# Splitting two weight halves with one instruction in the expert stage of a three-layer kernel

## The chip, the cores and the metric

The kernel runs on one core of a Trainium2 chip. The metric is the device time of one execution in microseconds. The kernel before was timed three times, and the median counts. A separate execution was taken with the hardware profiler; all durations below come from that one.

## The reference

One sequence of 256 tokens with 1024 features passes through three layers: a hybrid layer with four token mixers and a dense feed-forward block, a retention layer with a dense feed-forward block, and a Fourier layer with a mixture of eight experts. The last block is the one that matters here:

```python
logits = t @ w_router                          # 256 x 8
top_val, top_idx = lax.top_k(logits, 2)        # two experts for each token
top_w = softmax(top_val)
for e in range(8):
    out = out + gates[:, e:e + 1] * ((silu(t @ w_gate[e]) * (t @ w_up[e])) @ w_down[e])
```

Each expert has a gate and an up matrix of 1024 x 3584 and a down matrix of 3584 x 1024, all in float32. Its weights are 44 MB, and those of all eight, 352 MB, are most of what the kernel reads.

## The kernel before, in words

All weights lie in memory as units of 128 x 2048 float32 numbers, 1 MiB each, in the order of their use. There are `NU` units; the last 8 x 42 belong to the experts. SyncE's queue (SP) loads unit after unit into raw places, tiles named `raw`: six from the start, four more before the second dense block (`raw2p`), two more before the Fourier mixer (`raw3p`) and two more before the experts (`raw4p`). In the expert stage the tile `xT` serves as one more. So 15 units can be loaded ahead there. A raw place is given back, and its next load issued, when VectorE (DVE) has finished the second half of the unit.

TensorE multiplies in a rounded float32 format, so each weight is split into a rounded part and a remainder. `split()` does that for half a unit, 128 x 1024: ScalarE (ACT) copies `raw` to `wh` with rounding (L128), then DVE writes `wl = raw - wh` (L129). `wh` and `wl` come from the pool `wp` with four buffers each, so four halves at most are split and not yet used up. The list `wq` holds halves that wait for use. `half()` first splits one more half (unless told `ahead=False`), then takes the oldest from `wq`.

The orders of TensorE (PE) and SP are as the code writes them. Those of ACT and DVE are made by a scheduler from priorities, and each engine then runs its list in order.

The experts: `experts()` (from L1115) walks seven strips of 512 hidden columns. A strip takes 12 halves: four for the gate projection (`gate_strip`, L1142 to L1144), four for the up projection (`up_strip`), four for the down projection of the strip before (`down`). In `gate_strip` every half is fetched by a `nexth()` of its own; in `up_strip` and `down` two are fetched by `pair()`, which splits one half before the matmuls and one after. ScalarE takes the silu of the gate strip (`sg`, L1177), DVE multiplies it by the up strip (`h`, L1184), `turn()` transposes that on PE (`sd`, L1194 or L1196), and ACT and DVE split the result into `hx` (L1200, L1201). An expert with at most 64 tokens takes the packed form for up, down and the transposes: both parts of the tokens' numbers lie side by side in one stationary operand (L1139 and L1144), 4 matmuls for a half and not 6. The gate strips always take 6.

Around the experts, `gather()` builds the tokens of the next expert: selection matrices `so` on DVE (L1082), `rows` on PE (L1093), `xs` on ACT (L1095), `tokens_of` on PE (L1100), `ex` on ACT and DVE (L1102, L1103), and `rest` on PE (L1108, L1110), which reads the row scale `rcol` and feeds `rsl` and `sot` (L1111, L1112). These steps are hooked into the last seven halves of the expert before. `result()` splits an expert's output into `y`, and `combine()` adds it to `acc` during the next expert.

Of the kernel before, what the change touches and what calls it, by code (L numbers as in the profile page):

```python
# [9 lines left out]
F32 = mybir.dt.float32  # L10
F32R = mybir.dt.float32r
I32 = mybir.dt.int32
AF = mybir.ActivationFunctionType
ALU = mybir.AluOpType
AX = mybir.AxisListType

P = 128
# [5 lines left out]
E = 8  # L23
FE = 3584
NFE = FE // P
UN = 2048
UE = 42
# [36 lines left out]
def kernel(  # L64
# [10 lines left out]
    nc = tc.nc  # L75
    NU = ws_d.shape[0]
    WB = 4
    HP = 300
    HQ = 512
    HU = UN // 2  # L80

    NRAW, R2N, R3N, R4N = 6, 4, 2, 2
    const = ctx.enter_context(tc.tile_pool(name="const", bufs=1))
    rawp = ctx.enter_context(tc.tile_pool(name="rawp", bufs=NRAW))
    wp = ctx.enter_context(tc.tile_pool(name="wp", bufs=WB))
    psp = ctx.enter_context(tc.tile_pool(name="psp", bufs=2, space=bass.MemoryType.PSUM))
    ctx.enter_context(tc.manual_schedule(engines={mybir.EngineType.PE, mybir.EngineType.SP}))

# [1 line left out]
    raw = []  # L90
    wq = []
# [18 lines left out]
    def more_room(name, n):  # L110
        pool = ctx.enter_context(tc.tile_pool(name=name, bufs=n))
        for _ in range(n):
            fetch(pool)

    half_ = [0, 0]

    def split(scales=None, between=None):


        if not raw or (half_[1] == H_F2 and scales is None):  # L120
            return
        half_[1] += 1
        r = raw[0][0][:, half_[0] * HU:(half_[0] + 1) * HU]
        wh = wp.tile([P, HU], F32R, tag="wh", name="wh")
        wl = wp.tile([P, HU], F32R, tag="wl", name="wl")
        if scales is None:
            for o in (slice(0, HQ), slice(HQ, HU)) if half_[1] == 1 else (slice(0, HU),):
                nc.scalar.activation(out=wh[:, o], in_=r[:, o], func=AF.Copy)  # L128
                nc.vector.tensor_tensor(out=wl[:, o], in0=r[:, o], in1=wh[:, o].bitcast(F32), op=ALU.subtract)  # L129
                if between is not None and o.start == 0:  # L130
                    between()
        else:
            for t in range(2):
                o = slice(t * 512, t * 512 + 512)
                nc.scalar.activation(out=wh[:, o], in_=r[:, o], func=AF.Copy, scale=scales[:, t:t + 1])
                nc.vector.scalar_tensor_tensor(out=wl[:, o], in0=r[:, o], scalar=scales[:, t:t + 1],
                                               in1=wh[:, o].bitcast(F32), op0=ALU.mult, op1=ALU.subtract)
        wq.append((wh, wl))
        if half_[0]:
            fetch(raw.pop(0)[1])  # L140
        half_[0] ^= 1
# [29 lines left out]
    def half(ahead=True):  # L171

        for item in list(side):
            item[0] -= 1
            if item[0] <= 0:
                advance(item)
        if ahead:
            split()
        return wq.pop(0)
# [6 lines left out]
    def mm3T(ps, u, b, xh, xl, start, stop):  # L186
        wh, wl = u
        c = slice(b * P, (b + 1) * P)
        mm(ps, wh[:, c], xh, start=start, stop=False)  # L189
        mm(ps, wh[:, c], xl, start=False, stop=False)  # L190
        mm(ps, wl[:, c], xh, start=False, stop=stop)  # L191
# [10 lines left out]
    def unit_late(xh, xl, late=2):  # L202

        ps = [bank("mm", (P, S)) for _ in range(2)]
        us = []
        for cb in range(2):
            us.append(half())
            for k in range(KD - late):
                mm3T(ps[cb], us[cb], k, xh[:, k], xl[:, k], k == 0, False)
        for cb in range(2):  # L210
            for k in range(KD - late, KD):
                mm3T(ps[cb], us[cb], k, xh[:, k], xl[:, k], False, k == KD - 1)
        return ps

    def stripX(xh, xl, mid=None):
# [157 lines left out]
    with pa:  # L373
# [9 lines left out]
        def hilo(dst, j, src):  # L383
# [11 lines left out]
                                in1=col(C_N1, 8).unsqueeze(2).to_broadcast([P, KD, 4]), op=ALU.mult)  # L395
# [342 lines left out]
    with ExitStack() as pr:  # L738
# [120 lines left out]
        for c in range(KD):  # L859
            ps = bank("mm", (P, S))  # L860
            for j in range(16):
                if j % 8 == 0:
# [16 lines left out]
                            in1=col(C_FFN1, 8).unsqueeze(2).to_broadcast([P, KD, E]), op=ALU.mult)  # L879
    th = xh.rearrange("p (t a) s -> p t (a s)", t=2)  # L880
    tl = xl.rearrange("p (t a) s -> p t (a s)", t=2)
    if R3N:
        more_room("raw3p", R3N)
    with ExitStack() as pn:
        N = pn.enter_context(tc.tile_pool(name="N", bufs=1))
        zh = N.tile([P, KD, S], F32R, name="zh")
# [124 lines left out]
        for c in range(0, KD, 2):  # L1011
            ps, o = to_tok(xT_, c, "mm")
# [46 lines left out]


    pt.close()
    if R4N:
        more_room("raw4p", R4N)
    xT_flat = xT.rearrange("p a b -> p (a b)")
    fetch(xT_flat)
    fn = xT_flat[:, 0:D]
    with ExitStack() as pe:
# [48 lines left out]
        def experts(ex, rs, half_fn, hooks=None, n_of=None):  # L1116
# [10 lines left out]
            def nexth(**kw):  # L1127
                if hooks and n[0] in hooks:
                    hooks[n[0]]()
                n[0] += 1  # L1130
                return half_fn(**kw)
# [76 lines left out]
            def down(s, mid=None):  # L1208
                def blocks(b0):
                    pair(lambda w, packed: hi_lo(ht[s], [down_item(s, b0 + i, w[i], hf) for i in range(2) for hf in range(2)],  # L1210
                                                 packed))

                blocks(0)
                if mid is not None:
                    mid()
                if s < 6:
                    blocks(2)
                else:

                    w = [nexth() for _ in range(2)]  # L1220
                    for hf in range(2):
                        either(lambda packed: hi_lo(ht[s], [down_item(s, b, w[b - 2], hf) for b in (2, 3)], packed))
                        with tc.high_priority(HP):
                            result(hf)

            res = []

            def result(hf):
                y = G2.tile([P, 2, 512], F32R, tag="hx", name="y")
                yh, yl = y[:, 0], y[:, 1]  # L1230
                nc.scalar.activation(out=yh, in_=pd[hf], func=AF.Copy)
                nc.vector.tensor_tensor(out=yl, in0=pd[hf], in1=yh.bitcast(F32), op=ALU.subtract)
                res.append((yh, yl))
# [30 lines left out]
        for i in (0, 2, 1, 3):  # L1264
            nxt[3][i]()
        finish_rms()
        last = None
        for e in range(E):
            ex, sot, rs, _ = nxt
# [34 lines left out]
        with tc.tile_pool(name="O", bufs=1) as O:  # L1304
            ecur = O.tile([P, E], F32, name="ecur")
            emask = O.tile([P, E], F32, name="emask")
            epos = O.tile([P, 2], F32, name="epos")
            egts = O.tile([P, 2], F32, name="egts")
            etmp = O.tile([P, 2, E], F32, name="etmp")
            with tc.If(n_over[0] + n_over[1] > 0):  # L1310

                nc.vector.tensor_copy(out=ecur, in_=io8)
                with tc.For_i(0, E, 1) as ev:
                    nc.vector.tensor_scalar(out=emask, in0=ecur, scalar1=-8.0, scalar2=None, op0=ALU.is_equal)
                    for src, dst in ((pos, epos), (gts, egts)):
                        nc.vector.tensor_tensor(out=etmp, in0=src, in1=emask.unsqueeze(1).to_broadcast([P, 2, E]), op=ALU.mult)
                        nc.vector.tensor_reduce(out=dst, in_=etmp, axis=AX.X, op=ALU.add)
                    nc.vector.tensor_scalar(out=epos, in0=epos, scalar1=float(-P), scalar2=None, op0=ALU.add)
                    cnt_ = [0]
                    cur_ = []  # L1320

                    def ohalf(ahead=True):
                        i, h = divmod(cnt_[0], 2)
                        if h == 0:
                            t = rawp.tile([P, UN], F32, tag="raw", name="oraw")
                            nc.sync.dma_start(t, ws_d[bass.ds(ev * UE + (NU - E * UE + i), 1)].rearrange("a p n -> p (a n)"))
                            cur_[:] = [t]
                        r = cur_[0][:, h * HU:(h + 1) * HU]
                        wh = wp.tile([P, HU], F32R, tag="wh", name="owh")
                        wl = wp.tile([P, HU], F32R, tag="wl", name="owl")  # L1330
                        nc.scalar.activation(out=wh, in_=r, func=AF.Copy)
                        nc.vector.tensor_tensor(out=wl, in0=r, in1=wh.bitcast(F32), op=ALU.subtract)
                        cnt_[0] += 1
                        return wh, wl

                    oex, osot, ors, steps = gather(lambda t: epos[:, t:t + 1], lambda t: epos[:, t:t + 1])
                    for f in steps:
                        f()
                    combine(experts(oex, ors, ohalf), osot, lambda t: egts[:, t:t + 1])
                    nc.vector.tensor_scalar(out=ecur, in0=ecur, scalar1=-1.0, scalar2=None, op0=ALU.add)  # L1340
                for hf in range(2):
                    out_sumsq(hf)
                out_rms()
# [172 lines left out]
```

## Time and profile before

| what | value |
|---|---|
| time, median of 3 (all: 1871.12, 1874.76, 1873.32) | 1873.32 us |
| time of the profiled execution | 1872.74 us |
| its span, first to last instruction | 1871.0 us |
| PE busy | 1817.4 us (97%) |
| DVE busy | 1482.0 us (79%) |
| ACT busy | 1210.6 us (65%) |
| mean DMA rate over the span | 270 GB/s |

The page gives each engine's busy time over the whole span. These are means over stages that differ: up to about 895 us the three layers' dense work, then the experts to about 1856 us, then the final norm. The expert stage is read from windows, one for an expert. The packed form of an expert shows in its number of matmuls. A line group of the trace gives a mean duration, which for DVE and ACT is longer than the distance of two such instructions that follow each other, since the next starts before the last has ended; that distance is read from the rows of a timeline.

### The profile page before, as it was taken

Reading aid. Unit: us, or ns where it says so; the run is one execution under the profiler, and the core shown is the slowest. Engines: PE = TensorE matmul, PEld = TensorE weight load, DVE = VectorE, ACT = ScalarE, POOL = GpSimd, SP = SyncE. Lnnn points to the kernel's source line nnn. Section 1 sums busy time; section 2 is a strip of 40 time slices with the busy share of each in tenths; the row PEclk is TensorE's granted clock in tenths of the full one; section 3 lists DMA queues with packets and bytes.
Section 4 is the critical chain, followed back from the end, with each engine's and each line's share of the span. In section 5 each row is a group of like instructions: output and inputs, shape, how many; then the busy total and the mean of one; then the engine's idle time right before and its main releaser. Section 6 shows DMA issues by size and latency. Waiting matters only on the chain. (4 is left out here: it accounts for less than half of the span.)

```text
span 1871.0 us, 28740 instructions
## 1 busy us (share of the span) xinstructions
PE 1817.4 (97%) x10890; PEld 1574.5 (84%) x10890; DVE 1482.0 (79%) x1855; ACT 1210.6 (65%) x1484; POOL 158.2 (8%) x154
## 2 busy tenths in 40 slices
PE   8999999999999999999999999999999999999997
PEld 7999999999888999998777887777777788888885
DVE  5666676657677666656899989999999998988987
ACT  5765454455344444446787777888878777777775
POOL 2302122211111122110000000000000000000000
PEclk9999999999999999999999999999999999999999
DMA  8344544555444564544799998999999999999970
GB/s 313 140 154 168 193 178 183 181 181 197 158 150 159 189 248 184 187 170 180 295 419 377 353 367 326 411 386 377 415 354 413 381 353 364 332 356 354 343 290 36
DMA packets 71156, 505.77 MB, mean 270 GB/s; under 512 B 7888, under 2 KB 8016, under 8 KB 10320
## 3 DMA queue, kind: packets, MB, share of 16 engines
q1 hardware_dynamic: 70992, 503.53, 70.7%
q8 instruction: 110, 1.80, 0.4%
q14 instruction: 54, 0.44, 0.1%
HBM read 502.45 MB, written 1.05 MB: 269 GB/s over the span
## 5 line engine op out<-in xcount | busy, mean ns | idle before, releaser
L129 DVE TENSOR_TENSOR wl<-raw,wh 128x1024 fp32r<-128x1024 f32 (+1 forms) x906 | 1078.5, 1227 | 235.3 <-ACT wh L128 226.2
L128 ACT ACTIVATE wh<-raw 128x1024 fp32r<-128x1024 f32 (+1 forms) x906 | 922.0, 1053 | 428.9 <-PE mm L190 188.7
L189 PE MATMUL mm<-xh,wh 128*128 128x256 f32 x1248 | 357.5, 286 | 6.7 <-ACT xh L342 6.7
L1144 PE MATMUL mm<-wl,ex 128*128 128x512 f32 x896 | 356.0, 397 | 3.7 <-DVE wl L129 3.7
L190 PE MATMUL mm<-xl,wh 128*128 128x256 f32 x1248 | 355.2, 285 | 1.0 <-DVE xl L343 0.7
L191 PE MATMUL mm<-xh,wl 128*128 128x256 f32 x1248 | 354.9, 284 | 0.8 <-DVE wl L129 0.8
L1142 PE MATMUL mm<-wh,ex 128*128 128x512 f32 x672 | 270.4, 402 | 0.0
L1143 PE MATMUL mm<-wh,ex 128*128 128x512 f32 x672 | 266.1, 396 | 0.2 <-DVE ex L1103 0.2
L189 PEld LDWEIGHTS mm<-xh,wh 128*128 128x128 f32 x1248 | 237.9, 191 | 8.2 <-ACT xh L342 6.7
L190 PEld LDWEIGHTS mm<-xl,wh 128*128 128x128 f32 x1248 | 237.9, 191 | 2.4 <-DVE xl L343 2.3
L191 PEld LDWEIGHTS mm<-xh,wl 128*128 128x128 f32 x1248 | 237.7, 190 | 1.1 <-DVE wl L129 1.0
L1144 PEld LDWEIGHTS mm<-wl,ex 128*128 128x128 f32 x896 | 168.6, 188 | 54.2 <-DVE wl L129 13.7
L1144 PE MATMUL dn<-wl,hx 128*128 128x512 f32 x448 | 183.6, 410 | 12.1 <-DVE wl L129 11.9
L1143 PEld LDWEIGHTS mm<-wh,ex 128*128 128x128 f32 x672 | 126.7, 189 | 28.2 <-DVE ex L1103 0.5
L1142 PEld LDWEIGHTS mm<-wh,ex 128*128 128x128 f32 x672 | 126.6, 188 | 26.0 <-ACT wh L128 0.3
L1144 PEld LDWEIGHTS dn<-wl,hx 128*128 128x128 f32 x448 | 84.2, 188 | 55.8 <-DVE wl L129 40.1
L190 PE MATMUL mm<-hl,wh 128*128 128x256 f32 x352 | 99.8, 283 | 0.0
L191 PE MATMUL mm<-hh,wl 128*128 128x256 f32 x352 | 99.8, 283 | 0.0
L189 PE MATMUL mm<-hh,wh 128*128 128x256 f32 x352 | 99.8, 283 | 0.0
L1139 PE MATMUL dn<-wh,hx 128*128 128x512 f32 x224 | 89.2, 398 | 0.0
L1142 PE MATMUL dn<-wh,hx 128*128 128x512 f32 x224 | 88.9, 397 | 0.0
L1139 PE MATMUL mm<-wh,ex 128*128 128x512 f32 x224 | 88.7, 396 | 0.0
(400 smaller groups left out, 2500.7 us busy)
## 6 DMA issues: line engine op xcount, KB each, us to landing
raw<-in_ws_dram SPq DMA_DIRECT2D x451, 1024.0 KB, 6.3
xT<-in_ws_dram SPq DMA_DIRECT2D x22, 1024.0 KB, 7.0
raw<-in_ws_dram SPq DMA_DIRECT2D x3, 512.0 KB, 6.3
xT<-in_xT_dram SPq DMA_DIRECT2D x4, 256.0 KB, 5.4
xT<-in_xT_dram SPq DMA_DIRECT2D x1, 1024.0 KB, 8.3
out_dram<-acc SPq DMA_DIRECT2D x4, 256.0 KB, 2.1
cstA<-in_cst_dram SPq DMA_DIRECT2D x1, 576.0 KB, 9.1
raw<-in_ws_dram SPq DMA_DIRECT2D x2, 256.0 KB, 4.5
```

Source lines behind the costliest of these rows:

```text
L128: nc.scalar.activation(out=wh[:, o], in_=r[:, o], func=AF.Copy)
L129: nc.vector.tensor_tensor(out=wl[:, o], in0=r[:, o], in1=wh[:, o].bitcast(F32), op=ALU.subtract)
L189: mm(ps, wh[:, c], xh, start=start, stop=False)
L190: mm(ps, wh[:, c], xl, start=False, stop=False)
L191: mm(ps, wl[:, c], xh, start=False, stop=stop)
L1139: mm(out_, e, wh, start=first, stop=False)
L1142: mm(out_, e, wh, start=first, stop=False)
L1143: mm(out_, xk[:, P:2 * P], wh, start=False, stop=False)
L1144: mm(out_, e, wl, start=False, stop=last)
```

## The change

From the fifth half of the experts on (`H_MOE + WB`), `split()` treats a whole unit: one ACT instruction and one DVE instruction of 128 x 2048, into one of four places that stay for the whole stage, each with room for a unit's `wh` and `wl`. Two of them are the old four buffers, now one tile each (`ringh`, `ringl`), two are new (`place0`, `place1`). The call of `split()` that would have split the unit's second half does nothing. Before the experts start, `wq` is filled to six halves (a unit's two halves join together), and the next unit is split when one more unit has been used up. The raw pools `raw3p` and `raw4p`, four buffers, go. In the earlier stages halves are split as before, into the four parts of the ring. Where two halves are in use at once (`unit_late`, and the end of `down`), the second `split()` is moved behind their matmuls. The final unit is split in halves, since it is loaded in halves.

```diff
-    NRAW, R2N, R3N, R4N = 6, 4, 2, 2
+    NRAW, R2N = 6, 4
-    wp = ctx.enter_context(tc.tile_pool(name="wp", bufs=WB))
+    wp = ctx.enter_context(tc.tile_pool(name="wp", bufs=1))
+
+    ring = [wp.tile([P, WB, HU], F32R, name=f"ring{n}") for n in "hl"]
+    H_MOE = 2 * (NU - E * UE)
+    places = [[r.rearrange("p a n -> p (a n)")[:, i * UN:(i + 1) * UN] for r in ring] for i in (0, 1)]
+    if H_MOE % WB:
+        places.reverse()
...
+        if half_[1] >= H_MOE + WB:
+
+            r, pool = raw[0]
+            wide = half_[1] < 2 * NU - 2
+            if not (wide and half_[0]):
+                wh, wl = places[(half_[1] - H_MOE) // 2 % 4]
+                o = slice(0, UN) if wide else slice(half_[0] * HU, (half_[0] + 1) * HU)
+                nc.scalar.activation(out=wh[:, o], in_=r[:, o], func=AF.Copy)
+                nc.vector.tensor_tensor(out=wl[:, o], in0=r[:, o], in1=wh[:, o].bitcast(F32), op=ALU.subtract)
+                for i in range(2) if wide else half_[0:1]:
+                    wq.append((wh[:, i * HU:(i + 1) * HU], wl[:, i * HU:(i + 1) * HU]))
+                if wide or half_[0]:
+                    raw.pop(0)
+                    fetch(pool)
+            half_[0] ^= 1
+            half_[1] += 1
+            return
+        wh, wl = (r[:, half_[1] % WB] for r in ring)
         half_[1] += 1
         r = raw[0][0][:, half_[0] * HU:(half_[0] + 1) * HU]
-        wh = wp.tile([P, HU], F32R, tag="wh", name="wh")
-        wl = wp.tile([P, HU], F32R, tag="wl", name="wl")
...
-            us.append(half())
+            us.append(half(ahead=not cb))
...
+        split()
         return ps
...
-    if R3N:
-        more_room("raw3p", R3N)
...
-    if R4N:
-        more_room("raw4p", R4N)
+    wp3 = ctx.enter_context(tc.tile_pool(name="wp3", bufs=1))
+    for i in range(2):
+        places.append([wp3.tile([P, UN], F32R, name=f"place{i}{n}") for n in "hl"])
...
-                    w = [nexth() for _ in range(2)]
+                    w = [nexth(), nexth(ahead=False)]
...
+                    if half_fn is half:
+                        split()
...
         finish_rms()
+        while len(wq) < 6:
+            split()
```

PE's list is the same row for row. ACT's and DVE's lists change at three places that matter below.

Place one is a strip in the middle of an expert, on ACT. `hx` is the transposed product of the strip before, `sg` the silu of this strip's gate part, and the rows L128 or L135 are splits; a branch is the end of a packed-or-not section on PE. ACT before:

```order
L1200 ACTIVATE hx_10568<-sd_10558 128x4x128
L128 ACTIVATE wh_10596<-raw_10158 128x1024
L128 ACTIVATE wh_10621<-raw_10158 128x1024
L1177 ACTIVATE sg_10593<-mm_10535,rsl_9952 128x512
L1150 UNCONDITIONAL_BRANCH
L128 ACTIVATE wh_10627<-raw_10177 128x1024
L1150 UNCONDITIONAL_BRANCH
L128 ACTIVATE wh_10652<-raw_10177 128x1024
L128 ACTIVATE wh_10660<-raw_10212 128x1024
```

And ACT now:

```order
L1222 ACTIVATE hx_9760<-sd_9750 128x4x128
L1199 ACTIVATE sg_9779<-mm_9733,rsl_9387 128x512
L135 ACTIVATE place1h_9369<-raw_9484 128x2048
L1172 UNCONDITIONAL_BRANCH
L135 ACTIVATE ringh_64<-raw_9554 128x2048
L1172 UNCONDITIONAL_BRANCH
L135 ACTIVATE ringh_64<-raw_9579 128x2048
L1172 UNCONDITIONAL_BRANCH
L135 ACTIVATE place0h_9367<-raw_9592 128x2048
L135 ACTIVATE place1h_9369<-raw_9621 128x2048
```

Between `hx` and `sg` two half splits stood, and now none does. On DVE the same strip has six halves between `hx` and `h` and six between `h` and the next `hx`, and now three units and three units.

Place two is the end of the first expert on DVE, where the next expert's tokens (`ex`, `so`, `rsl`, `sot`) are made. DVE before:

```order
L1201 TENSOR_TENSOR hx_11268<-sd_11258,hx_11268 128x4x128
L1103 TENSOR_TENSOR ex_10002<-sd_11275,ex_10002 128x4x128
L129 TENSOR_TENSOR wl_11317<-raw_10843,wh_11316 128x1024
L1150 UNCONDITIONAL_BRANCH
L129 TENSOR_TENSOR wl_11342<-raw_10843,wh_11341 128x1024
L1103 TENSOR_TENSOR ex_10002<-sd_11347,ex_10002 128x4x128
L1150 UNCONDITIONAL_BRANCH
L129 TENSOR_TENSOR wl_11355<-raw_10876,wh_11354 128x1024
L1150 UNCONDITIONAL_BRANCH
L1111 COPY rsl_10004<-sd_11358 128x1
```

And DVE now:

```order
L1223 TENSOR_TENSOR hx_10478<-sd_10468,hx_10478 128x4x128
L1125 TENSOR_TENSOR ex_9447<-sd_10481,ex_9447 128x4x128
L1172 UNCONDITIONAL_BRANCH
L1133 COPY rsl_9449<-sd_10552 128x1
L1134 CAST sot_9448<-sd_10552 128x256
L1104 TENSOR_SCALAR so_11750<-cst_73,pos_9294 128x64
L1104 TENSOR_SCALAR so_11750<-cst_73,posu_9295 128x64
L136 TENSOR_TENSOR place1l_9370<-raw_10223,place1h_9369 128x2048
L1172 UNCONDITIONAL_BRANCH x2
L1125 TENSOR_TENSOR ex_9447<-sd_10545,ex_9447 128x4x128
```

Three half splits stood between the first `ex` and `rsl`, and now none does. At the other six handovers a unit stands before and a unit behind the first `ex`, and `rsl` comes after `y`.

Place three is the start of the first expert on DVE. The rows L311 to L318 compute the row scale `rcol` step by step, `so` selects tokens. DVE now:

```order
L314 TENSOR_SCALAR rsy_9421<-rsh_9418 128x2
L136 TENSOR_TENSOR place0l_9368<-raw_8514,place0h_9367 128x2048
L316 SCALAR_TENSOR_TENSOR rs1_9417<-rsy_9421 128x2
L1104 TENSOR_SCALAR so_9442<-cst_73,pos_9294 128x64
L317 TENSOR_TENSOR rs1_9417<-rs1_9417,rs0_9416 128x2
L1104 TENSOR_SCALAR so_9442<-cst_73,posu_9295 128x64
L318 SCALAR_TENSOR_TENSOR rsy_9421<-rs1_9417,rsy_9421 128x2
L136 TENSOR_TENSOR place1l_9370<-raw_8568,place1h_9369 128x2048
L1125 TENSOR_TENSOR ex_9385<-sd_9402,ex_9385 128x4x128
```

Before, no split stood between these rows; the first four halves of the expert were split during the Fourier layer's last matmuls, as they still are, and the next came after both `ex`.

## Rows read from the trace of the kernel before

**Rows 1.** Windows, one an expert: busy us of each engine, granted clock, DMA share, GB/s.
```profile
1010.30:1136.50 126.20, 125.73 (x560) 101.05 (x559) 113.18 (x113) 95.00 (x105) 0.00 (x0) 1.00 0.95 353
1250.30:1364.00 113.70, 108.27 (x480) 81.99 (x480) 111.42 (x112) 93.16 (x105) 0.00 (x0) 1.00 0.97 388
```

**Rows 2.** Line groups, experts: busy us, mean ns; idle before, releasers.
```profile
L129 DVE TENSOR_TENSOR wl<-raw,wh 128x1024 fp32r<-128x1024 f32 x623 | 728.3, 1221 | 59.6 <-ACT wh L128 56.1 <-PE mm L1144 0.2
L128 ACT ACTIVATE wh<-raw 128x1024 fp32r<-128x1024 f32 x624 | 626.3, 1053 | 147.1 <-PE mm L1143 83.5 <-PE dn L1142 34.6 <-PE mm L1142 12.9
...
L1201 DVE TENSOR_TENSOR hx<-sd,hx 128x512 fp32r<-128x512 f32 x56 | 38.5, 688 | 0.3
...
L1194 PE MATMUL sd<-cst,h 128*128 128x128 f32 x224 | 30.1, 278 | 4.0 <-DVE h L1184 4.0
```

**Rows 3.** Timeline of DVE over one packed strip: start us, us, engine, line, xcount.
```profile
1302.46 7.12 DVE L129 TENSOR_TENSOR wl<-raw,wh 128x1024 fp32r<-128x1024 f32 x6
1309.50 0.75 DVE L1184 SCALAR_TENSOR_TENSOR h<-mm,rsl,sg 128x512 f32<-128x512 f32 x1
1310.16 5.76 DVE L129 TENSOR_TENSOR wl<-raw,wh 128x1024 fp32r<-128x1024 f32 x5
1315.84 1.22 DVE L129 TENSOR_TENSOR wl<-xT,wh 128x1024 fp32r<-128x1024 f32 x1
1317.07 0.69 DVE L1201 TENSOR_TENSOR hx<-sd,hx 128x512 fp32r<-128x512 f32 x1
1317.68 1.22 DVE L129 TENSOR_TENSOR wl<-xT,wh 128x1024 fp32r<-128x1024 f32 x1
```

**Rows 4.** Timeline of PE over the same strip.
```profile
1299.81 1.05 PE L1194 MATMUL sd<-cst,h 128*128 128x128 f32 x8
1300.62 0.48 PE L1142 MATMUL mm<-wh,ex 128*128 128x512 f32 x1
...
1303.51 0.39 PE L1139 MATMUL mm<-wh,ex 128*128 128x512 f32 x1
...
1307.23 0.40 PE L1139 MATMUL dn<-wh,hx 128*128 128x512 f32 x1
...
1311.43 0.50 PE L1144 MATMUL dn<-wl,hx 128*128 128x512 f32 x1 [0.60 <-DVE wl L129]
```

**Rows 5.** Timeline of ACT over the same strip.
```profile
1304.44 0.67 ACT L1177 ACTIVATE sg<-mm,rsl 128x512 f32<-128x512 f32 x1
1305.01 6.73 ACT L128 ACTIVATE wh<-raw 128x1024 fp32r<-128x1024 f32 x7
1313.60 1.06 ACT L128 ACTIVATE wh<-raw 128x1024 fp32r<-128x1024 f32 x1 [1.86 <-PE mm L1143]
```

**Rows 6.** Timeline of DVE around the first expert's start, instructions after idle time.
```profile
900.10 0.69 DVE L1103 TENSOR_TENSOR ex<-sd,ex 128x512 fp32r<-128x512 f32 x1 [2.63 <-ACT ex L1102]
...
910.99 2.36 DVE L129 TENSOR_TENSOR wl<-raw,wh 128x1024 fp32r<-128x1024 f32 x2 [1.72 <-ACT wh L128]
```

**Rows 7.** Timeline of DVE where the first expert hands over to the second.
```profile
1006.15 0.68 DVE L1103 TENSOR_TENSOR ex<-sd,ex 128x512 fp32r<-128x512 f32 x1
...
1009.10 1.23 DVE L129 TENSOR_TENSOR wl<-raw,wh 128x1024 fp32r<-128x1024 f32 x1 [1.14 <-ACT wh L128]
...
1011.39 1.22 DVE L129 TENSOR_TENSOR wl<-raw,wh 128x1024 fp32r<-128x1024 f32 x1 [0.26 <-ACT wh L128]
```

**Rows 8.** Timeline of PE at the same place.
```profile
1009.79 0.55 PE L1110 MATMUL sd<-rcol,so 128*128 128x1 f32 x4
```

**Rows 9.** Windows: the initial loads, and a packed expert's strips.
```profile
15.00:35.00 20.00, 18.13 (x108) 15.62 (x107) 14.30 (x27) 10.18 (x15) 6.78 (x7) 1.00 1.01 423
1300.00:1320.00 20.00, 19.40 (x90) 15.05 (x90) 19.84 (x20) 16.96 (x20) 0.00 (x0) 1.00 1.02 418
```

**Rows 10.** Waits of SP's queue, 1200 to 1500 us: total us, times, longest.
```profile
SPq L101 <- DVE wl L129: 257.4, 111, 4.3
```

**Rows 11.** The loads of line 101: their times to landing.
```profile
DMA to landing us min/median/max: 4.3/6.4/16.8
```

More of the change, by code (lines that the diff above doesn't have):

```diff
@@ L1328, in ohalf @@
                         r = cur_[0][:, h * HU:(h + 1) * HU]
-                        wh = wp.tile([P, HU], F32R, tag="wh", name="owh")
-                        wl = wp.tile([P, HU], F32R, tag="wl", name="owl")
+                        wh, wl = (x[:, cnt_[0] % WB] for x in ring)
                         nc.scalar.activation(out=wh, in_=r, func=AF.Copy)
```

## The prediction

> **What bounds the kernel now.** I read the windows first, one for each expert. A row gives the stretch, its length, the busy time of PE, PEld, DVE, ACT and POOL, the granted clock of PE, the DMA share and the rate. Two kinds of expert appear [rows 1]. An unpacked one lasts 126.2 us and PE works 125.7 us of it, so nothing that DVE saves can shorten it. A packed one lasts 113.7 us; PE works 108.3 us and DVE 111.4 us. How many are packed follows from the line groups [rows 2]: `turn()` has 8 matmuls on L1194 in a packed strip, and 224 = 4 experts x 7 strips x 8. The change must therefore earn its keep in four experts, at their handovers and at the start.
>
> Next come the timelines of one packed strip, the same 15 us on three engines. On DVE [rows 3] a strip repeats from 1302.46 to 1317.68, which is 15.22 us. It holds 12 half splits, `h` (1310.16 - 1309.50 = 0.66) and `hx` (0.61), so 15.22 - 1.27 = 13.95 us for the halves, 1.163 each. Where five stand in a row without any wait, their distance is (1315.84 - 1310.16) / 5 = 1.136. Twelve at that pace are 13.63 us, so 0.32 us of the strip is waiting. On PE [rows 4] the transposes take 0.81 us, a gate unit (1303.51 - 1300.62) 2.89, and two packed units (1307.23 - 1303.51) 3.72. A strip of two gate units and four packed units needs 0.81 + 5.78 + 7.44 = 14.03 us, and the late rows of the group show PE waiting for `wl` (0.60 us at 1311.43). So DVE sets the pace of a packed strip, and PE follows 1.2 us behind. ACT [rows 5] splits a half in (6.73 - 1.06) / 6 = 0.945 us and waits for PE to give buffers back (1.86 us).
>
> **The change part by part.** Merging two DVE splits. The trace has no DVE instruction of 2048 columns. Two shapes give its slope: 688 ns at 512 and 1221 ns at 1024 columns [rows 2] are 1.041 ns a column. If a wider instruction only adds columns, its distance to the next is 1.136 + 1.066 = 2.20 us, against 2 x 1.136 = 2.27 before: 0.07 us a unit. From below, the saving may be nothing or slightly negative (the two distances just add up, or the longer operand rows cost a little); from above it is the whole part of the duration that doesn't grow with columns, 1.221 - 1.066 = 0.155 us. I take 0.07, since distance and not duration is what fills a strip.
>
> [...]
>
> A strip after the change is then 6 x 2.20 + 1.27 = 14.47 us on DVE, if it never waits: 0.75 us less than now, of which 12 x 1.136 - 6 x 2.20 = 0.43 comes from merging and 0.32 from waits that vanish. There are 6 whole strips between handovers in each packed expert, 24 in all: 18.0 us.
>
> Look-ahead. Four halves can be split and unused now; then six can, in four places of two halves, and the split of a unit waits only for the end of the unit four before it. ACT's 1.9 us and DVE's 2.3 us stand against three units of PE, at least 5.6 us, so the waits for buffers on PE [rows 5] should go. But each split now comes as a lump. `sg` waits for PE to finish the gate strip, and one unit of `down` is split by ACT behind it, 0.67 + 1.9 us later; DVE can then only start that unit. DVE needs work for that time, and PE has 3.72 + 1.86 = 5.58 us of other units before it wants this one, against 0.67 + 1.9 + 2.3 = 4.9 us. That is narrow, so I keep a third of the 7.8 us of waits: -2.6 us.
>
> The other six units of each packed expert lie about its handover; there only the merge counts, 4 x 6 x 0.07 = 1.7 us.
>
> The first expert's start. DVE idles 2.63 and 1.72 us there [rows 6], and two more halves or units are now split in those gaps. The first gap can be filled by the unit that the fill to six halves puts there, if ACT has split it by then; a table load on ACT and the small rows of `rcol` lie between. The gain is 0 to 4.35 us. I take half, 2.2.
>
> The end of the first expert. DVE's list now has `rsl` right behind the first `ex`; `rsl` waits for `rest` on PE, and splits stand behind it. The first `ex` ends by 1006.8 [rows 7] and `rest` at 1010.2 [rows 8], so DVE stands idle for 3.4 us, against 1.14 + 0.26 = 1.40 before: -2.0 us. The second expert is bound by PE, but PE wants the units that DVE has not split. The look-ahead of six halves may hide part of it; its bounds are 0 and 3.4. The other handovers have a unit between and I leave them as they are.
>
> Fewer raw places. 15 places become 11. SP's queue waits for DVE to free a place at practically every load, 111 times in 300 us [rows 10], so loads are issued as soon as a place is free. At a strip's pace of 2.41 us a unit, 11 places leave 26.5 us from that issue until DVE wants the unit. The landing takes 6.4 us in the median and 16.8 at most [rows 11], and ACT stands up to three units, some 6.5 us, before DVE: 3.2 us are left even then. The transfers themselves are the tighter point. A packed strip at 14.47 us asks for 6 x 1.049 MB = 435 GB/s, more than the 418 to 423 GB/s seen with a DMA share of 1 [rows 9]. The shortage is 14.98 - 14.47 = 0.5 us a strip, 3 us an expert, which the places can lend and the handover returns (a whole expert at 109 us asks for 44.04 MB / 109 = 404 GB/s). I cost it at nothing; without that cover it is rival A.
>
> [...]
>
> The narrow stages before the experts keep PE's order and a look-ahead of four halves. The moved second split in `unit_late` and `down` follows PE's matmuls by less than a half's use: 0, within 1 us either way. Unpacked experts: 0, since PE is busy all through.
>
> The sum: 18.0 - 2.6 + 1.7 + 2.2 - 2.0 = 17.3 us. The profiled execution took 1872.74 us, its span of 1871.0 and 1.7 around it, and lies 0.6 us below the median of the runs. 1872.74 - 17.3 = 1855.4 us.
>
> **The rivals.** A: the transfers become the bound of a packed strip. For it speak the rates above and the four places fewer. Against it, no wait of ACT names a load in the experts now. A strip then takes 14.98 us, 24 x 0.24 = 5.8 us gained; the gain at the start stays and the loss at the first handover is covered: 1872.7 - 5.8 - 2.2 + 0.3 for the refill = about 1865 us.
>
> [...]
>
> B: no change. Merging saves nothing, since two distances simply add up, and the waits on DVE stay because the two units of one ring tile are ordered as one tile. Nothing in the rows excludes the second; against the first speaks the slope of [rows 2]. 4.35 us at most at the start and up to 3.4 lost at the handover leave 1871 us, give or take 2.
>
> C: slower. The split is a lump, and `sg` stands ahead of it in ACT's list, where two halves were between `hx` and `sg` before. The round then runs: gate strip on PE 5.78, `sg` 0.67, ACT 1.9, DVE 2.3, the last unit on PE 1.86, transposes 0.81, in all 13.3 us, with some 0.4 for passing between engines 13.7, under 14.47. If two units stand behind `sg` and not one, DVE adds 2.2: 15.9 us a strip, above the 15.22 of now. It decides from there on: 24 x 0.7 = 16.8 us slower, 1872.7 + 16.8 - 2.2 + 2.0 = about 1889. Against it, the list shows the look-ahead already filled when `sg` comes.
>
> **How the numbers follow.** My forecast has a chance of 0.62, A 0.13, B 0.14, C 0.11. The forecast's own range is 1846 to 1864: all waits gone and 0.12 us a merge on the low side, no waits gone and half the merge on the high side. PE's 14.03 us a strip limits any gain there to 24 x 1.19 = 28.6 us, and 1872.7 - 28.6 = 1844 is the low end. The high end takes in A and most of B: 1873. What a measurement can tell from no change is 0.2%, 3.7 us: faster is below 1869.6 and slower above 1877.1. Faster: 0.62 + 0.13 = 0.75, with B's lower tail set against the forecast's upper one. The same: 0.13. Slower: 0.12, C and a remainder of B.
>
> **What would show it.** Right: wide `wl` instructions with a mean of 2.29 us and a distance of 2.20; packed experts of about 109 us beside unpacked ones of 126; DVE without idle time in a packed strip; `rsl` of the first handover behind 3 us of idle time; no ACT wait on a load. Wrong: ACT's splits waiting for transfers, with a DMA share of 1 through whole experts (A); strips of 15.2 us with waits on PE for places (B); DVE idle behind ACT once a strip, and PE behind DVE at the last unit of `down` (C); wide distances of 2.27 or more would halve the gain.

## The result, and the profile after

The changed kernel takes 1888.59 us in the median of four runs (1887.05 to 1889.1), the kernel before 1873.5: a ratio of 1.0081, with a 95% interval of 1.0063 to 1.0098. It is slower by 15 us, and 1855.4 was forecast. The profiled execution has a span of 1886.7 us against 1871.0, 15.7 more.

To see where, I cut both traces at the first `sg` of each expert, as ACT's timeline has it. Two of the experiments told below stand beside them.

| stretch, us | before | after | e8 | e5 |
|---|---|---|---|---|
| start to the first `sg` | 909.3 | 914.6 | 912.0 | 909.2 |
| expert 0 (packed) | 110.3 | 105.6 | 117.6 | 106.3 |
| expert 1 | 126.2 | 126.6 | 125.1 | 126.6 |
| expert 2 (packed) | 113.7 | 117.7 | 117.8 | 108.7 |
| expert 3 (packed) | 113.7 | 118.2 | 118.2 | 109.1 |
| expert 4 (packed) | 113.0 | 117.9 | 118.0 | 108.8 |
| experts 5 and 6 | 251.8 | 251.4 | 251.3 | 251.3 |
| expert 7 to the end | 132.9 | 134.7 | 134.4 | 134.4 |

A handover is the stretch from an expert's last `sg` to the next expert's first. Expert 0 gained 4.7 us, which the later start took back. Experts 2 to 4 lost 13.4 us, and the end 1.8. The unpacked ones are as they were. The packed experts are thus of two kinds after the change, which the windows show as well (length, then busy us of PE, PEld, DVE, ACT and POOL, granted clock, DMA share, GB/s; expert 3, an unpacked one, expert 0):

```profile
1264.50:1382.70 118.20, 108.90 (x479) 82.47 (x479) 108.78 (x71) 87.94 (x62) 0.00 (x0) 1.00 0.97 373
1500.60:1626.40 125.80, 125.33 (x563) 101.81 (x563) 110.09 (x71) 88.85 (x62) 0.00 (x0) 1.00 0.95 356
914.60:1020.20 105.60, 100.99 (x459) 81.01 (x458) 99.59 (x65) 86.37 (x62) 0.00 (x0) 0.98 0.99 398
```

In expert 3 DVE has 108.8 us of work, less than the 111.4 of before [rows 1], and yet the expert is 4.5 us longer than before: DVE waits. The wide instructions themselves are what was forecast, 2287 ns against 2 x 1221 [rows 2]:

```profile
L136 DVE TENSOR_TENSOR ringl<-raw,ringh 128x2048 fp32r<-128x2048 f32 x152 | 344.6, 2287 | 39.1 <-ACT ringh L135 39.0
L135 ACT ACTIVATE ringh<-raw 128x2048 fp32r<-128x2048 f32 x152 | 285.7, 1909 | 10.0 <-PE mm L1165 9.0
```

The two timelines of a strip of expert 3 show what DVE waits for. They answer to [rows 3] and [rows 5]. Below, G0 and G1 are a strip's gate units, U0 and U1 its up units, D0 and D1 those of the down projection. ACT first; its six rows are `hx`, U1, `sg`, D0, D1 and the next `hx`:

```profile
1308.47 0.60 ACT L1222 ACTIVATE hx<-sd 128x512 fp32r<-128x512 f32 x1 [3.73 <-PE sd L1216]
1308.97 1.91 ACT L135 ACTIVATE ringh<-raw 128x2048 fp32r<-128x2048 f32 x1
1311.23 0.69 ACT L1199 ACTIVATE sg<-mm,rsl 128x512 f32<-128x512 f32 x1 [0.36 <-PE mm L1166]
1311.82 1.91 ACT L135 ACTIVATE place0h<-raw 128x2048 fp32r<-128x2048 f32 x1
1313.62 1.91 ACT L135 ACTIVATE place1h<-raw 128x2048 fp32r<-128x2048 f32 x1
...
1324.69 0.60 ACT L1222 ACTIVATE hx<-sd 128x512 fp32r<-128x512 f32 x1 [3.76 <-PE sd L1216]
```

DVE over the same strip: `hx`, U1, D0, D1, `h`, and then G0 and G1 of the next:

```profile
1309.25 0.69 DVE L1223 TENSOR_TENSOR hx<-sd,hx 128x512 fp32r<-128x512 f32 x1
1310.91 2.29 DVE L136 TENSOR_TENSOR ringl<-raw,ringh 128x2048 fp32r<-128x2048 f32 x1 [0.97 <-ACT ringh L135]
1313.76 2.29 DVE L136 TENSOR_TENSOR place0l<-raw,place0h 128x2048 fp32r<-128x2048 f32 x1 [0.56 <-ACT place0h L135]
1315.97 2.28 DVE L136 TENSOR_TENSOR place1l<-raw,place1h 128x2048 fp32r<-128x2048 f32 x1
1318.17 0.75 DVE L1206 SCALAR_TENSOR_TENSOR h<-mm,rsl,sg 128x512 f32<-128x512 f32 x1
1318.83 4.49 DVE L136 TENSOR_TENSOR ringl<-raw,ringh 128x2048 fp32r<-128x2048 f32 x2
```

And PE, which waits for G0 at the end of that row's first unit:

```profile
1321.17 0.50 PE L1166 MATMUL mm<-ringl,ex 128*128 128x512 f32 x1 [0.50 <-DVE ringl L136]
```

ACT stands idle for 3.73 us in front of `hx`, which needs the transposes on PE, while U1's place is free. Then `sg` needs the whole gate strip, and both D units stand behind it. On DVE this puts back the start of U1 by 1.05 us (1310.91 - 1309.25 - 0.61) and that of D0 by 0.65 (1313.76 - 1310.91 - 2.20), together 1.7 us a strip. From there a ring of waits closes: `sg` and D0 on ACT (1311.23 to 1313.76), D0, D1, `h` and the next G0 on DVE (to 1321.17), the rest of G0 on PE (2.43), transposes (0.81) and G1 (3.08 to the next `sg`, 1327.49). That is 16.26 us, the strip. In expert 0 the list on ACT is another one. There D0 stands ahead of `hx` and only D1 behind `sg`:

```profile
961.98 1.92 ACT L135 ACTIVATE place0h<-raw 128x2048 fp32r<-128x2048 f32 x1 [0.35 <-PE mm L1165]
963.81 0.58 ACT L1222 ACTIVATE hx<-sd 128x512 fp32r<-128x512 f32 x1
965.86 0.69 ACT L1199 ACTIVATE sg<-mm,rsl 128x512 f32<-128x512 f32 x1 [1.48 <-PE mm L1166]
966.44 1.91 ACT L135 ACTIVATE place1h<-raw 128x2048 fp32r<-128x2048 f32 x1
```

DVE has no idle time in that strip, and D0, D1 and the next G0 follow each other at 2.20 us:

```profile
967.33 2.29 DVE L136 TENSOR_TENSOR place0l<-raw,place0h 128x2048 fp32r<-128x2048 f32 x1
969.53 2.29 DVE L136 TENSOR_TENSOR place1l<-raw,place1h 128x2048 fp32r<-128x2048 f32 x1
971.73 2.29 DVE L136 TENSOR_TENSOR ringl<-raw,ringh 128x2048 fp32r<-128x2048 f32 x1
```

Once PE has used up its lead, expert 0's last strips take 14.54 and 14.39 us, the 14.47 of the forecast. From the third strip of expert 1 on the scheduler's list is the one of expert 3.

### The profile page after: what moved, and what is told of

The parts are those of the page before. It is cut to its first block, busy times and chain, and to the rows that moved or that the text cites. A ratio compares the mean times of both kernels' runs of the same rounds, so it can differ in the third digit from the quotient of the medians.

```text
span 1886.7 us, 27702 instructions
## 1 busy us (share of the span) xinstructions
PE 1815.9 (96%) x10890; PEld 1581.4 (84%) x10890; DVE 1457.7 (77%) x1522; ACT 1166.7 (62%) x1151; POOL 158.3 (8%) x154
## 3 DMA queue, kind: packets, MB, share of 16 engines
HBM read 502.45 MB, written 1.05 MB: 267 GB/s over the span
## 5 line engine op out<-in xcount | busy, mean ns | idle before, releaser
L151 DVE TENSOR_TENSOR ringl<-raw,ringh 128x1024 fp32r<-128x1024 f32 (+1 forms) x282 | 349.2, 1239 | 180.3 <-ACT ringh L150 171.8
L150 ACT ACTIVATE ringh<-raw 128x1024 fp32r<-128x1024 f32 (+1 forms) x282 | 295.9, 1052 | 290.4 <-PE mm L212 192.2
L136 DVE TENSOR_TENSOR ringl<-raw,ringh 128x2048 fp32r<-128x2048 f32 x152 | 344.6, 2287 | 39.1 <-ACT ringh L135 39.0
L211 PE MATMUL mm<-xh,ringh 128*128 128x256 f32 x1248 | 357.5, 286 | 7.1 <-ACT xh L365 7.1
L213 PE MATMUL mm<-xh,ringl 128*128 128x256 f32 x1248 | 355.0, 284 | 1.4 <-DVE ringl L151 1.4
L212 PE MATMUL mm<-xl,ringh 128*128 128x256 f32 x1248 | 355.4, 285 | 1.0 <-DVE xl L366 0.7
L135 ACT ACTIVATE ringh<-raw 128x2048 fp32r<-128x2048 f32 x152 | 285.7, 1909 | 10.0 <-PE mm L1165 9.0
L211 PEld LDWEIGHTS mm<-xh,ringh 128*128 128x128 f32 x1248 | 238.1, 191 | 8.6 <-ACT xh L365 7.1
L212 PEld LDWEIGHTS mm<-xl,ringh 128*128 128x128 f32 x1248 | 238.0, 191 | 2.2 <-DVE xl L366 2.1
L136 DVE TENSOR_TENSOR place0l<-raw,place0h 128x2048 fp32r<-128x2048 f32 x76 | 173.8, 2287 | 13.0 <-ACT place0h L135 11.6
L135 ACT ACTIVATE place0h<-raw 128x2048 fp32r<-128x2048 f32 x76 | 145.5, 1914 | 6.8 <-PE mm L1165 3.3
L135 ACT ACTIVATE place1h<-raw 128x2048 fp32r<-128x2048 f32 (+1 forms) x77 | 145.5, 1889 | 1.9 <-PE mm L1165 1.9
L1164 PE MATMUL mm<-ringh,ex 128*128 128x512 f32 x344 | 138.1, 401 | 0.0
L1165 PE MATMUL mm<-ringh,ex 128*128 128x512 f32 x344 | 136.0, 395 | 0.7 <-DVE ex L1125 0.7
L1166 PEld LDWEIGHTS mm<-ringl,ex 128*128 128x128 f32 x448 | 84.1, 188 | 31.2 <-DVE ringl L136 11.8
```

What stands on the lines that cost most here:

```text
L1164: mm(out_, e, wh, start=first, stop=False)
L1165: mm(out_, xk[:, P:2 * P], wh, start=False, stop=False)
L1166: mm(out_, e, wl, start=False, stop=last)
```

## The experiments

The theory (O): the position of the splits in ACT's list decides. Its rivals: the wide instruction as a lump (L), and the four raw places fewer (R). The table gives ACT's list from one `sg` to the next and the length of a settled strip; a half is marked, all else are whole units.

| kernel, packed experts | behind `sg`, in ACT's list | split in | strip, us |
|---|---|---|---|
| before, all | D0 D1 G0 G1 U0 `hx` U1 | halves | 15.22 |
| after, expert 0 | D1 G0 G1 U0 U1 D0 `hx` | units | 14.5 |
| after, experts 2 to 4 | D0 D1 G0 G1 U0 `hx` U1 | units | 16.22 |
| e1 and e5 | D1 G0 G1 U0 U1 `hx` D0 | units | 14.47 |
| e2, experts 2 to 4 | U1 D0 D1 G0 G1 U0 `hx` | halves | 16.70 |
| e3 and e6 | D1 G0 G1 U0 U1 `hx` D0 | halves | 14.88 |
| e4, expert 2 | D0 D1 G0 G1 U0 `hx` U1 | halves | 15.22 |
| e4, expert 4 | U1 D0 D1 G0 G1 half of U0 `hx` half of U0 | halves | 16.77 |
| e8, all four | D0 D1 G0 G1 U0 `hx` U1 | units | 16.23 |

DVE's list, which the scheduler makes, moves a little too: U1 stands behind `hx` in experts 2 to 4 after the change and in e8, and ahead of it in e5. In e4, DVE's list is the same in the settled strips of experts 2 and 4, and these strips still differ by 1.55 us (15.22 and 16.77). There ACT's list alone is at work.

In the edits below, the names of engines are shortened, and lines that the text tells in words or that only move are left out.

**e1, wide, ACT in written order.** From the changed kernel:

```diff
+        manual.enter_context(tc.manual_schedule(engines={PE, SP, Activation}))
         last = None
         for e in range(E):
```

> Edit: the changed kernel, with ACT's instructions of the expert stage kept in the order in which the code writes them (hx behind the split of U1, the split of D0 ahead of sg) instead of the scheduler's. Nothing else is changed. Theory O (order): the changed kernel lost its time because from the second expert on ACT's list puts hx ahead of U1's split and sg ahead of both D splits, so that DVE idles 0.97 and 0.56 us a strip. Then the strips of experts 2 to 4 fall from 16.22 to 14.5 us and the whole to about 1861 us (1857 to 1866). Theory L (lump): an instruction twice as long holds up ACT and DVE wherever it stands; strips stay at 15.9 or above, the whole at 1884 or above. Theory R (raw places): the four places fewer make loads late; ACT or DVE would wait for loads and strips lie at 15 or above, the whole at 1872 or above.

It took 1872.51 us, a ratio of 1.0000 to before (0.9991 to 1.0008). The strips are 14.47 us, as O has it. The total misses by 11 us: with `xs`, `ex` and `y` in written order too, the stretch from the last `sg` of an expert to the next grew from 22.7 to 24.9 us, and the first whole strip from 14 to 16.5. The strips were right, the handovers not thought of. In e1's trace PE waits 7.3 us for `hx` before L1115, the next tokens' `rows` (four waits, 1.9 at most), and 6.9 us for `acc` before the transposes of L1216 (three, 2.4 at most); e5's trace shows neither. The granted clock of e1's executions is 0.987 to 0.990, that of e5's 0.993 to 0.994.

**e2, halves, the scheduler's order.**

```diff
-            wide = half_[1] < 2 * NU - 2
-            if not (wide and half_[0]):
+            wide = False
+            if True:
```

> Edit: the changed kernel, with each unit split by two instructions of 1024 columns again, in the same four places and with the same look-ahead of six halves; ACT's order is the scheduler's, which from the third strip of the second expert on puts hx and sg ahead of U1 and both D units. Theory O: the order costs as much as with wide instructions. The round sg 0.6, U1's first half on ACT 0.95, then on DVE U1, both D units, h and G0 of the next strip (2.27 + 4.54 + 0.66 + 2.27), then the rest of G0, the transposes and G1 on PE (1.4 + 0.81 + 2.89) is 16.4 us: strips of 16 to 16.5, the whole 1882 to 1893. Theory L: without the lump the strip is 15.2 or less, the whole 1874 or less.

1902.39 us, a ratio of 1.016 (1.0146 to 1.0174), strips of 16.70 us. Without any wide instruction it is the slowest of all. L alone cannot explain the loss. O's ring gave 16.4 us for this list. The strip and the total are both above O's ranges, 16 to 16.5 us and 1882 to 1893; what that excess is made of stays open.

**e3, halves, ACT in written order** (both edits).

> Edit: as the run before (two instructions of 1024 columns for a unit, four places, look-ahead of six halves), but with ACT's instructions of the expert stage in the order in which the code writes them. Theory O: DVE never waits in a strip, which is 12 x 1.136 + 1.27 = 14.9 us; the whole is about 1870 us (1866 to 1874), some 8 to 10 us above the wide instructions in the same order, which is what merging is worth (0.07 us a unit). Theory L: it is faster than the wide instructions in the same order.

1868.44 us, 0.9976 (0.9966 to 0.9986), strips of 14.88 us as worked out. That it came out under e1 is L's forecast, but the strips say otherwise, 14.88 against 14.47; the difference lies at the handovers again. e5 and e6 settle that.

**e4, the kernel before with 11 places to load into.**

```diff
-    NRAW, R2N, R3N, R4N = 6, 4, 2, 2
+    NRAW, R2N, R3N, R4N = 6, 4, 0, 0
```

> Edit: the kernel before, without the two pools of two raw places each, so that 11 units and not 15 can be loaded ahead in the expert stage. Theories O and L: no change, 1870 to 1877 us, strips of packed experts still 15.22 us. Theory R: at least 8 us slower, ACT's splits waiting for loads in the packed experts.

1887.02 us, 1.0073 (1.006 to 1.0086): O and L missed, and R's number came. Its mechanism did not. Experts 0 to 2 are the same as before to 0.1 us, and from the fifth strip of expert 3 on ACT's list is a later one, though no instruction of ACT was changed. In expert 4 (`sg`, `hx`, `sg` on ACT, then two DVE rows) DVE waits for ACT and not for a load:

```profile
1425.36 0.69 ACT L1177 ACTIVATE sg<-mm,rsl 128x512 f32<-128x512 f32 x1 [1.26 <-PE mm L1144]
...
1439.33 0.60 ACT L1200 ACTIVATE hx<-sd 128x512 fp32r<-128x512 f32 x1 [0.51 <-PE sd L1194]
...
1442.13 0.69 ACT L1177 ACTIVATE sg<-mm,rsl 128x512 f32<-128x512 f32 x1 [1.26 <-PE mm L1144]
```

```profile
1427.03 2.37 DVE L129 TENSOR_TENSOR wl<-xT,wh 128x1024 fp32r<-128x1024 f32 x2 [1.67 <-ACT wh L128]
...
1443.80 2.36 DVE L129 TENSOR_TENSOR wl<-raw,wh 128x1024 fp32r<-128x1024 f32 x2 [1.67 <-ACT wh L128]
```

Experts 3 and 4, where the list is the later one, hold 12.3 of the 14 us (3.6 and 8.7); the other 1.6 had come before the experts. So four raw places fewer cost most of this by way of the order, as far as the rows show; no run gave this kernel the earlier list back. The loads keep up: e3 and e5 run faster on the same 11 places. How the scheduler comes to the later list was not looked into.

**e5, wide, only the strips in written order.**

```diff
             for s in range(1, 7):
+                with ExitStack() as manual:
+                    if half_fn is half:
+                        manual.enter_context(tc.manual_schedule(engines={PE, SP, Activation}))
+                    gate_strip(s, lambda: turn(s - 1))
+                    if s < 6:
+                        up_strip(s)
+                        down(s - 1)
+                if s == 6:
+                    up_strip(s)
+                    down(s - 1, lambda: turn(6))
```

> Edit: the changed kernel, with ACT in the order of the code only inside the strips 1 to 6 of each expert (up to the gate part of the sixth); at the handovers the scheduler's order stays, with xs, ex and y ahead of the splits. Theory O (order): strips of experts 2 to 4 at 14.47 us as in the run with the written order everywhere, but with the changed kernel's handovers (22.7 us from the last sg to the next, not 24.9) and first strips (14 and not 16.5). A packed expert then takes 14 + 5 x 14.47 + 22.7 = 109 us, the whole 1888.5 - 3 x 9 = 1861 us (1857 to 1866). Rival (transfers): 6.29 MB in 14.47 us is 435 GB/s, more than the 418 to 423 seen; without the longer handovers the loads don't catch up, splits wait for loads from the third expert on and the strips lie at 15 us: 1867 or above.

1857.96 us, 0.9915 (0.9901 to 0.9929): faster than both kernels, 2.6 us from the forecast for the change. DVE's strip, from `hx` to `hx`, is 1309.81 - 1295.34 = 14.47 us and has no idle time:

```profile
1295.34 0.69 DVE L1223 TENSOR_TENSOR hx<-sd,hx 128x512 fp32r<-128x512 f32 x1
...
1301.01 4.49 DVE L136 TENSOR_TENSOR ringl<-raw,ringh 128x2048 fp32r<-128x2048 f32 x2
...
1309.81 0.69 DVE L1223 TENSOR_TENSOR hx<-sd,hx 128x512 fp32r<-128x512 f32 x1
```

Two windows of it, 40 us of strips and the whole of expert 3, show the transfers at a DMA share of 1.01 and 1.00, with 418 and 405 GB/s, and still in time:

```profile
1280.00:1320.00 40.00, 39.01 (x175) 31.07 (x175) 40.00 (x24) 34.29 (x23) 0.00 (x0) 1.00 1.01 418
1250.70:1359.80 109.10, 104.98 (x479) 83.56 (x478) 107.67 (x71) 88.21 (x63) 0.00 (x0) 1.00 1.00 405
```

**e6, halves, only the strips in written order** (the edits of e2 and e5).

> Edit: as the run before, but every unit is split by two instructions of 1024 columns. Theory O: strips of 14.88 us as with the halves in written order, handovers of 23 to 24: 1868 to 1872 us, so merging is worth 0.4 us a strip, 24 strips, some 10 us, once the order is the same. If the halves come out at or below the wide instructions, merging is worth nothing by itself.

1869.77 us, 0.9976 (0.9967 to 0.9985). DVE's strip from `h` to `h` is 14.88 us:

```profile
1295.48 0.75 DVE L1206 SCALAR_TENSOR_TENSOR h<-mm,rsl,sg 128x512 f32<-128x512 f32 x1
...
1310.36 0.75 DVE L1206 SCALAR_TENSOR_TENSOR h<-mm,rsl,sg 128x512 f32<-128x512 f32 x1
```

On the same chip, with the same list on ACT in the settled strips, the merge is worth 1869.77 - 1857.96 = 11.8 us. In the two traces the four packed experts are 9.5 us apart (1.6, 2.8, 2.5 and 2.6); a settled strip differs by 0.41.

**e7, e5 with DVE's start in written order.**

```diff
+        with tc.manual_schedule(engines={PE, SP, DVE}):
+            nxt = gath(0)
+            finish_rms()
+            for i in (0, 2, 1, 3):
+                nxt[3][i]()
+            while len(wq) < 6:
+                split()
```

> Edit: as the first of these three; besides, DVE's instructions between the last routing steps and the first expert stand in written order with the row scale and ex ahead of the two units that fill the look-ahead. The changed kernel lost 1.1 us at the start of the first expert and 3.3 at the first handover, where rsl stood in front of all splits on DVE for 3.57 us. Theory: the first ex no longer waits behind a 2.2 us split, and rsl stands behind y again; 2 to 4 us under the first run: 1857 to 1860 us. Rival: DVE's idle time at the start is spent anyway, and the splits that come later there are late in the first strips: no change against the first run, or up to 3 us more.

1858.95 us, 0.9916 (0.9902 to 0.993), no different from e5, as the rival had it. The end of expert 0 did shorten, from 25.4 to 21.6 us from `sg` to `sg`, since DVE's list changed there too (the reason stands with the first handover below). But the first `sg` came 7.7 us later in the trace: 4.7 of it had built up before the experts, and 3.0 at their start.

**e8, the bad list by hand.** e5, but without the fill to six halves, and with a hook `2: lambda: [split() for _ in range(2)]` in the first expert. The look-ahead is then one unit shorter, and the written order itself is that of the changed kernel's experts 2 to 4, with DVE's list the same as well.

> Edit: as the run with the strips of ACT in written order, but the look-ahead is not filled before the first expert; two calls of split stand in a hook of its third half, which leaves the look-ahead one unit shorter from then on. In the code's own order U1's split then stands behind hx and both D splits behind sg, in every packed expert, the first one too: the list that the scheduler made for the changed kernel's experts 2 to 4. Theory O: what counts is where the splits stand in ACT's list, not who made it. Strips of all four packed experts at 16.2 us; the first expert, 105.6 us in the changed kernel, takes 112 to 116; the whole 1890 to 1900 us. Rival: the strips of 16.2 come from something else that differs between the first and the later experts (loads, places); the first expert then keeps its 14 to 14.5 us, the whole 1884 to 1890.

1894.65 us, 1.011 (1.0095 to 1.0126). All four packed experts have strips of 16.23 us, expert 0 too (117.6 us, where 112 to 116 had been given), and ACT waits in front of its `hx` as expert 3 did after the change:

```profile
985.32 0.60 ACT L1222 ACTIVATE hx<-sd 128x512 fp32r<-128x512 f32 x1 [3.74 <-PE sd L1216]
985.81 1.91 ACT L135 ACTIVATE place1h<-raw 128x2048 fp32r<-128x2048 f32 x1
988.12 0.69 ACT L1199 ACTIVATE sg<-mm,rsl 128x512 f32<-128x512 f32 x1 [0.40 <-PE mm L1166]
```

That is the closest test of the cause: the same instructions, one unit later in ACT's list, are 37 us apart (e5 and e8, each against its own runs of before: -0.85% and +1.1%).

**e9, e5 with `rsl` behind G1's split at the first handover.**

```diff
+                    tc.add_manual_dep(c.ins, lasts[-1].ins.name, NoSync)
```

> Edit: as the run with the strips of ACT in written order, but at the first handover DVE's rsl stands behind the second ex and G1's split, by a dependency on that split. Theory: DVE's 3.57 us of idle time before rsl go, and with them 2 to 3 us of the first expert: its last stretch falls from 25.4 to about 22.5 us, the whole to 1855 us. Rival: rsl is late for sg or h of the second expert, whose first strip grows by as much: 1858.

1856.58 us, 0.9919 (0.9905 to 0.9933), the same as e5 within the measurement; the stretch stayed at 25.4 us. The idle time only found another owner, `so`, which waits for the same work on PE:

```profile
1010.29 0.26 DVE L1105 TENSOR_SCALAR so<-cst,pos 128x64 fp32r<-128x64 f32 x1 [3.56 <-PE sd L1133]
```

My theory of the handover was therefore wrong: the idle time on DVE stayed, and the total did not change.

## Why the prediction was wrong

The step that failed is in "Look-ahead", and again where rival C was set aside with "the list shows the look-ahead already filled when `sg` comes". The prediction let one unit of `down` stand behind `sg` and spread that over 24 strips. The list that I had read was expert 0's. In experts 2 to 4, 18 of the 24 strips, two stand there, and U1 behind `hx`. DVE waits 0.97 and 0.56 us a strip for ACT to split them, and a settled strip takes 16.22 us where 14.47 and some 0.1 of waits were forecast. That is rival C's condition, two units behind `sg`, and about its price: 15.9 us a strip and 1889 in all were given, at a chance of 0.11; 16.22 and 1888.6 were measured. The condition was to be read off the list of every packed expert.

C's path was not quite the one that ran, and its total is in part luck. C closed its round over the last unit of `down` and the whole gate strip on PE; the measured ring runs over `h` and the next G0 on DVE, and only the rest of the gate strip is on PE. And C charged 0.7 us to 24 strips, 16.8 us, where the trace has 13.4 lost in experts 2 to 4, 4.7 gained in expert 0, 5.3 lost before it and 1.8 at the end. No run shows the 0.4 us that C's round has for passing between engines, nor the 0.3 for the refill in A's sum; both were my estimates. In the strip of expert 3 above, DVE starts D0 0.03 us after ACT's split of it has ended (1313.73 to 1313.76), and PE starts on G0 0.05 us after DVE's (1321.12 to 1321.17).

Point by point:

- PE, unpacked experts: right, 126 us as before.
- The merge, 0.07 us a unit: right, with a distance of 2.20 us, and 11.8 us in all (e5 against e6) where 24 x 0.43 + 1.7 = 12.0 had been reckoned. That the two are so close is in part luck, since the traces place only 9.5 in the packed experts.
- Waits that vanish, 0.32 us a strip less a third: wrong. In expert 0 they vanished; in experts 2 to 4 1.75 us came in their place (16.22 - 14.47). Halves under the same list lose only 0.32 (the kernel before), so a lump does cost there; under the list of e5 it costs nothing. L is right in so far, and only together with O.
- Fewer raw places, 0: right for the loads (no wait of more than 0.6 us on one in the changed kernel), wrong for what they do to the list. In the kernel before, they alone came with a later list and 14 us (e4). Whether they or the merge turned the list of the changed kernel is not shown. Rival A is refuted: 14.47 us a strip ran for four strips at a time in e5, with 418 GB/s.
- The first expert's start, +2.2 us: wrong in sign. The first `sg` came 5.3 us later. By the starts of the same matmuls in both traces, some 3.3 us of that had built up on PE before the experts (at 885 us); the runs with the same code up to there have from -1.3 (e5) to 2.5 (e1), and e4, with the code of before, 1.7. So it varies between executions and is not put down to the change. The other 2 us (1.2 and 1.1 in e5 and e9) lie where the fill now stands; no run left out its two splits, so it is not shown that they cost this, and e7, which moves them behind the row scale, came later still. The idle time of [rows 6] is filled, but DVE then waits for ACT two units later,

```profile
910.53 2.29 DVE L136 TENSOR_TENSOR ringl<-raw,ringh 128x2048 fp32r<-128x2048 f32 x1 [1.18 <-ACT ringh L135]
917.14 2.29 DVE L136 TENSOR_TENSOR place0l<-raw,place0h 128x2048 fp32r<-128x2048 f32 x1 [1.51 <-ACT place0h L135]
```

- The first handover, -2.0 us: the loss is there, by another path. DVE's idle time in front of `rsl` came, 3.57 us where 3.4 were read from [rows 7, 8]:

```profile
1012.79 0.16 DVE L1133 COPY rsl<-sd 128x1 f32<-128x1 f32 x1 [3.57 <-PE sd L1132]
```

But by the starts of its matmuls PE lost 3.2 us before that idle time began (at 1009.2), and nothing in it. DVE's list in expert 0 has the first unit of the last down projection ahead of the last strip's `h`, and PE's transposes wait 2.50 us for `h`. Soon after that wait PE's granted clock is 0.50 for 3.4 us. DVE, PE and the window of that stretch:

```profile
1000.67 2.29 DVE L136 TENSOR_TENSOR ringl<-raw,ringh 128x2048 fp32r<-128x2048 f32 x1
1002.87 0.76 DVE L1206 SCALAR_TENSOR_TENSOR h<-mm,rsl,sg 128x512 f32<-128x512 f32 x1
1003.77 1.13 PE L1216 MATMUL sd<-cst,h 128*128 128x128 f32 x8 [2.50 <-DVE h L1206]
1004.90:1008.30 3.40, 3.40 (x11) 2.82 (x10) 3.40 (x3) 1.20 (x2) 0.00 (x0) 0.50 1.01 422
```

The wait makes 2.2 of the 3.2 us. The rest lies in the 3.4 us at a clock of 0.50, where `dn` matmuls start every 0.42 to 0.43 us (1005.84 to 1007.97), and every 0.23 before the wait and after 1009.7. e5 and e9 have `h` at the same place in DVE's list, the same wait (2.48 us) and 25.4 us. In e7 `h` stands ahead of that unit; PE waits 0.31 us, and the stretch takes 21.6 us:

```profile
1005.14 0.74 DVE L1206 SCALAR_TENSOR_TENSOR h<-mm,rsl,sg 128x512 f32<-128x512 f32 x1
1006.03 1.13 PE L1216 MATMUL sd<-cst,h 128*128 128x128 f32 x8 [0.31 <-DVE h L1206]
```

So the prediction priced a wait that cost nothing and missed one that did; `h` stands above the first row that place two shows. That the stretch grew by 2.2 us (23.2 to 25.4), near the 2.0 forecast, is luck. e7 moved other rows as well; no run moved `h` alone.

- The tail, taken as untouched: 2.3 us longer, told below.

## What to carry to other kernels

Where a scheduler orders an engine, read its list in every repetition of a loop, not in the first: the pattern drifts, and a change of buffers alone can move it. Look for what stands behind a waiting instruction: here U1, behind an `hx` that waited 3.73 us on ACT, left DVE idle for 0.97 us. Under the same list on ACT the longer instructions lost more here, 1.75 us a strip with units against 0.32 with halves; so fix the order first, then merge. Two changes in one (merge, fewer places) are told apart only when each runs alone under the same list.

## What the runs showed of the hardware that was not expected

After the last branch DVE goes on with the final norm. In the kernel before its first instruction there comes 0.8 us after the branch (1864.34, 1865.16), after the change 3.1 us (1877.80, 1880.89). The first row is of after, the second of before:

```profile
1880.89 1.42 DVE L1373 SCALAR_TENSOR_TENSOR acc<-acc,fr,xT 128x512 f32<-128x512 f32 x2 [4.12 <-DVEq L1336]
```

```profile
1865.16 2.74 DVE L1348 SCALAR_TENSOR_TENSOR acc<-acc,fr,xT 128x512 f32<-128x512 f32 x4 [1.84 <-DVEq L1310]
```

The other eight runs made from the changed kernel have 3.1 to 3.3 us there; e4, which shares the code of before, 0.81. In the changed kernel a transfer of the instruction queue falls into the gap, at about 1878.8 us; in the kernel before none does (the nearest start at 1862.6 and 1865.5). Whether the gap comes from that transfer is not shown: no run took it apart.
